# Softmax shares transposed in 32x32 blocks on VectorE and regrouped through DRAM, with query tiles of every fourth 32 tokens

## Chip, cores and metric

The kernel runs on one core of a Trainium2 chip. The metric is its device time in microseconds, as the median of repeated runs; a profiled execution of the same program supplies the trace. Five engines work side by side, each with a queue of its own that is worked off in order: PE (matmuls; its weight loads are listed apart as PEld), DVE (VectorE), ACT (ScalarE), POOL (GpSimd) and SP (SyncE, which issues nearly all DMAs).

## What is computed

One layer of a hybrid encoder, in fp32: 512 tokens with 16 meta tokens put ahead of them, width 2048. Cut to what matters:

```python
hn   = rmsnorm(h, pre_norm_g)                       # (528, 2048)
proj = einsum('bld,dc->blc', hn, w_in)              # w_in: 2048 x 6656
qa, ka, va, ga, qb, kb, vb, gb = split(proj)

# mixer A: 8 heads of 128 on 2 key/value heads, RMSNorm on q and k, axial rotary
s  = einsum('bkgqd,bksd->bkgqs', qa, ka) * scale
ya = softmax(s) @ va * silu(ga)

# mixer B: 8 heads, two softmaxes of 64 columns each, with a distance penalty
bias = -slope[h] * abs(qpos[:, None] - kpos[None, :])
a  = softmax(q1 @ k1.T * scale + bias) - lam * softmax(q2 @ k2.T * scale + bias)
yb = rmsnorm(a @ vb, subln_g) * (1 - lambda_init) * silu(gb)

y = einsum('blc,cd->bld', concatenate([ya, yb]), w_out)   # 2048 x 2048
return (h + rmsnorm(y, post_norm_g))[:, 16:, :]           # the 512 tokens
```

## The kernel before

**Numbers.** Every product of fp32 numbers is made of three products of shorter numbers: an operand x is split into `hi` (a copy with rounding on ACT, L335) and `lo` = x - hi (a subtraction on DVE, L338), and hi·hi, lo·hi and hi·lo are summed in PSUM. So one piece of work on PE is a triple of matmuls, recorded by the helper behind L61; transposes on PE are recorded by the one behind L64.

**Order.** The object `Lanes` (L42 to L103) writes PE's instructions in program order and keeps a clock of estimated microseconds. Attention is written as generators ("tasks"): each `yield` of a number asks to be continued so many estimated microseconds later, the numbers standing in the table `LAG` (L32). After each triple of the projection, `poll` lets one task that is due write its PE instructions. So PE's queue is projection work with attention's scores, transposes and products with V strewn in at chosen distances. Other engines are ordered by a scheduler, by priority; weight splits get a high one (L153 to L159). On SP the loads are kept in the order in which they are written.

**Weights.** `wload` takes a block of 128 x 1024 of w_in from DRAM into a staging buffer `st` (L149), from where ACT writes `wh` (L156) and DVE `wl` (L157). The pool has three buffers of each. In the background SP and POOL move blocks of w_out and sum them in DRAM (`ws`; `load` at L141, and accumulating DMAs that POOL issues at L785); the projection behind attention uses these sums to need fewer products. At the end `wlast` loads four blocks of w_out that are used as they are.

**Attention.** A query tile is 128 tokens in a row: `q[:, tq]`. For each head there are two halves of two tiles. Mixer B (`attention_B`, L484 to L526) and mixer A (`attention_A`, L573 to L615) do the same with one tile: scores into the PSUM tile `sc` (one buffer); DVE takes scale and distance and finds the row's extreme into `p` (L502, L601); ACT takes the exponential and the row's sum (L510, L604); DVE its reciprocal (L512, L605); POOL scales p by it (L515, L606); in B, DVE adds the second softmax with its weight (L517). The distance comes from one table `dist`, read at an offset `w0` that depends on the tile. `p` is 128 queries x 528 keys, and has six buffers; `room` holds a task back while they are taken.

**Products with V.** The product needs the shares the other way round, keys on the partitions. `p_times_v` (L437 to L479) has PE transpose each p: per half, eight transposes of 128 x 128 for the 512 tokens and two of 32 columns for the 16 meta keys, in three PSUM banks `tr`. From PSUM, ACT writes `ph` (L335) and DVE `pl` (L338), each in two pieces of 512 columns; the meta keys' shares go to `pm`, where POOL makes a copy of the hi part. Then come 13 matmuls of 256 queries: three for each of the four 128-token blocks of keys, and one for the meta keys. The two transposing banks and the products are separate steps with lags between them (`turnA/B`, `bankA/B`, `pvA/B`), and the whole task starts a lag `pA` or `pB` after the scores.

**End.** The output projection works in blocks of columns for two token tiles at a time; `third_done` closes one tile's third block, `last_block` the last one's, and `row_block` scales a block, adds the residual and stores it. `end` does this for the last two tiles, t = 0 and t = 1.

Of the kernel before, what the change touches and what calls it, by code (L numbers as in the profile page):

```python
# [31 lines left out]
LAG = dict(vals=3.5, bank=2.8, bankA=1.5, bankB=2.5, turnA=1.5, turnB=1.5, pvA=2.6, pvB=4.0, scB=3.0,  # L32
           pB=8.0, ss=6.0, qA=2.35, scA=5.4, pA=4.14, rope=10.2, head=3.85, fin=1.35, qn=1.4, norm=4.0, valsA=(10.0, 7.0),
# [73 lines left out]
def kernel(ctx: ExitStack, tc: tile.TileContext, xT, xn, xm, w_s, w_t, w_q, w_o,  # L107
# [78 lines left out]
    def xload(k):  # L186
        st = ap.tile([P, NT], F32, name="xs", tag="p", bufs=6)
# [165 lines left out]

    dist = ap.tile([P, DW], F16, name="dist", tag="dist", bufs=1)
    pad(ap, "dpad", 32)
    load(dist, dist_d[2])
# [4 lines left out]
    def queries_B(h, pss, after=nullcontext):  # L361
# [7 lines left out]
        l2 = ap.tile([P, SEQ], F32R, name="l2", tag="ql", bufs=4)  # L369
        with after():  # L370
            hi(q1[L], qf[L])
            hi(q2[U], qf[U])
            hi(q1[U], qf[L])
            hi(q2[L], qf[U])
            lo(l1[L], qf[L], q1[L])
            lo(l2[U], qf[U], q2[U])
            lo(l1[U], qf[L], q1[L])
            lo(l2[L], qf[U], q2[U])
# [36 lines left out]
    pv_last, p_live = [None], [0]  # L415
# [15 lines left out]
    def room(n):  # L431

        while p_live[0] + n > 6:
            yield 0.3
        p_live[0] += n

    def p_times_v(pts, v, done, gate_of):  # L437
# [3 lines left out]
        ph = ap.tile([P, TT, 2 * P], F32R, name="ph", tag="ph")  # L441
        pl = ap.tile([P, TT, 2 * P], F32R, name="pl", tag="pl")
        pm = ap.tile([96, 2 * P], F32R, name="pm", tag="pm")
        for b in range(2):
            if b:
                yield LAG["turn" + ab]
            tr = ptr.tile([P, 512], F32, name="tr", tag="tr")
            for i in range(2):
                c = NM + (2 * b + i) * P
                for j in range(2):  # L450
                    transpose(tr[:, (2 * i + j) * P:(2 * i + j + 1) * P],
                                        pts[j][:, c:c + P], ident)
            tv = tr.rearrange("p (c q) -> p c q", c=2)
            hi(ph[:, 2 * b:2 * b + 2, :], tv)
            lo(pl[:, 2 * b:2 * b + 2, :], tv, ph[:, 2 * b:2 * b + 2, :])
        yield LAG["bank" + ab]
        tr = ptr.tile([P, 512], F32, name="tr", tag="tr")
        for j in range(2):
            transpose(tr[:32, j * P:(j + 1) * P], pts[j][:, 0:32], ident)
        p_live[0] -= 2 * len(pts) if gate_of is None else len(pts)  # L460
        hi(pm[0:32], tr[0:32, :2 * P])
# [17 lines left out]
        done(o)  # L479

# [3 lines left out]
    def attention_B(h, qs, ks, v, v_task):  # L484
        o = ap.tile([P, SEQ], F32, name="oB", tag="f", bufs=4)
        last = None
        for half in range(2):
            pts = []
            for t in (2 * half, 2 * half + 1):
# [4 lines left out]
                yield from room(2)  # L494
# [709 lines left out]
```

## Time and profile before

| what | value |
|---|---|
| time, median of 3 runs | 916.49 us (916.39 to 916.67) |
| profiled execution: time / span | 915.9 us / 914.1 us |
| mean granted TensorE clock | 0.997 |
| DMA: bytes, mean rate | 149.86 MB, 164 GB/s |
| share of 16 DMA engines, SP's queue / POOL's queue | 43.2% / 10.8% |
| DRAM read / written | 140.55 MB / 41.94 MB |

How to read it: busy time is the sum of the instructions' durations, overlaps counted once. A matmul's duration is longer than the time by which it holds up the next one, since matmuls are pipelined; what one costs is read from the distance between starts. In a row of groups, the numbers behind the first bar are busy us and mean ns of one, and behind the second the idle time of the engine ahead of them, with what ended it. Rows of instructions have the start in us and the duration in us.

### The profile page before, as it was taken

To read this page: it belongs to the slowest core of one execution; us is meant where nothing else is said; L and a number is where in the kernel's file an instruction comes from. 1 tells how busy PE (TensorE), PEld (TensorE's weight loads), DVE (VectorE), ACT (ScalarE), POOL (GpSimd) and SP (SyncE) were. 2 spreads that over 40 slices of the span, in tenths; PEclk is the share of its full clock that TensorE was granted. 3 is DMA by queue.
4 is the path that set the end of the run, shared out by engine and by line. 5 is a ranking of instruction groups with operands and counts; after the bars stand their busy time and mean duration, and the time that the engine had idled before them with its cause. 6 is when DMAs were issued, how large, how long until landed. Compare 5 with 4: busy or idle time off the path is not lost.

```text
span 914.1 us, 14275 instructions
## 1 busy us (share of the span) xinstructions
PE 900.1 (98%) x5450; PEld 799.6 (87%) x5450; DVE 587.9 (64%) x1041; ACT 503.1 (55%) x877; POOL 121.3 (13%) x168
## 2 busy tenths in 40 slices
PE   9999999999999999999999999999999999999995
PEld 8999898998989989898998888998888888888884
DVE  6586675757557485575765374686554665876887
ACT  6565564737456384554744434565566565665552
POOL 0101111210201111011010011231111100000012
PEclk9999999999999999999999999999999999999998
DMA  9837636674848658484322332133212228979784
GB/s 338 288 125 205 166 124 174 175 187 128 236 129 206 175 159 217 117 237 124 102 73 70 104 106 79 48 104 115 82 58 93 81 81 287 304 260 323 251 250 176
DMA packets 52979, 149.86 MB, mean 164 GB/s; under 512 B 7920, under 2 KB 14960, under 8 KB 52528
## 3 DMA queue, kind: packets, MB, share of 16 engines
q1 hardware_dynamic: 48160, 132.18, 43.2%
q0 software_dynamic: 4608, 16.78, 10.8%
q8 instruction: 42, 0.69, 0.3%
q14 instruction: 25, 0.20, 0.1%
q10 hardware_dynamic: 144, 0.01, 0.0%
HBM read 140.55 MB, written 41.94 MB: 200 GB/s over the span
## 4 chain that ended last, share of the span: by engine, by line
PE 91%; DVE 5%; ACT 2%; issue 1%; DMA 1%; DVEq 0%; ACTq 0%
PE pd L61 60%; PE po L61 14%; PE sc L61 6%; PE pv L61 5%; PE tr L64 5%; DVE wl L157 1%; DVE y L1102 1%; DMA st<-in_w_o_dram 1%; PE hot L61 0%; PE ss L61 0%; DVE y L1026 0%; DVE p L601 0%; ACT wh L156 0%; DVE l L338 0%; DVE pl L338 0%
## 5 line engine op out<-in xcount | busy, mean ns | idle before, releaser
L61 PE MATMUL pd<-xh,wh 128*128 128x264 f32 (+1 forms) x992 | 333.7, 336 | 0.0
L61 PE MATMUL pd<-xl,wh 128*128 128x264 f32 (+1 forms) x992 | 323.4, 326 | 0.0
L61 PE MATMUL pd<-xh,wl 128*128 128x264 f32 (+1 forms) x992 | 323.3, 326 | 0.0
L156 ACT ACTIVATE wh<-st 128x1024 fp32r<-128x1024 f32 (+2 forms) x159 | 165.6, 1041 | 200.3 <-PE pd L61 76.4
L157 DVE TENSOR_TENSOR wl<-st,wh 128x1024 fp32r<-128x1024 f32 (+2 forms) x159 | 191.1, 1203 | 106.2 <-ACT wh L156 105.1
L61 PEld LDWEIGHTS pd<-xh,wl 128*128 128x128 f32 x992 | 186.6, 188 | 16.3 <-DVE wl L157 0.2
L61 PEld LDWEIGHTS pd<-xh,wh 128*128 128x128 f32 x992 | 187.1, 189 | 11.1 <-ACT wh L156 0.3
L61 PEld LDWEIGHTS pd<-xl,wh 128*128 128x128 f32 x992 | 187.6, 189 | 9.5
L510 ACT ACTIVATE p<-p,mx 128x528 f32<-128x528 f32 x64 | 46.9, 734 | 43.2 <-DVE mx L502 42.9
L338 DVE TENSOR_TENSOR pl<-tr,ph 128x512 fp32r<-128x512 f32 x64 | 43.3, 685 | 15.2 <-ACT ph L335 14.8
L64 PE MATMUL tr<-ident,p 128*128 128x128 f32 (+1 forms) x320 | 50.6, 272 | 1.8 <-DVE pl L338 0.7
L502 DVE CUSTOM_DVE_ANT_0 p<-sc,dist 128x528 f32<-128x528 f32 x64 | 44.9, 701 | 11.4 <-PE sc L61 11.0
L61 PE MATMUL pd<-wh,xh 128*128 128x512 f32 x128 | 51.1, 399 | 0.0
L61 PE MATMUL pd<-wl,xh 128*128 128x512 f32 x128 | 50.0, 391 | 0.0
L61 PE MATMUL pd<-wh,xl 128*128 128x512 f32 x128 | 49.9, 390 | 0.0
L335 ACT ACTIVATE ph<-tr 128x512 fp32r<-128x512 f32 x64 | 37.5, 590 | 21.3 <-PE tr L64 20.9
L64 PEld LDWEIGHTS tr<-ident,p 128*128 128x128 f32 (+1 forms) x320 | 36.9, 131 | 12.0 <-DVE pl L338 1.1
L517 DVE SCALAR_TENSOR_TENSOR p<-p,c 128x528 f32<-128x528 f32 x32 | 24.5, 766 | 31.6 <-POOL p L515 31.6
L785 POOL DMA_DIRECT2D ws<-in_w_o_dram x32 | 26.7, 834 | 123.3 <-DMA ws<-in_w_o_dram 66.1
L606 POOL TENSOR_SCALAR p<-p,smA 128x528 f32<-128x528 f32 x32 | 23.1, 721 | 137.6 <-DVE smA L605 99.3
L604 ACT ACTIVATE p<-p,mxA 128x528 f32<-128x528 f32 x32 | 23.5, 736 | 31.8 <-DVE mxA L601 31.1
L515 POOL TENSOR_SCALAR p<-p,sm 128x528 f32<-128x528 f32 x32 | 22.8, 714 | 137.1 <-DVE sm L512 126.1
(221 smaller groups left out, 1591.1 us busy)
## 6 DMA issues: line engine op xcount, KB each, us to landing
st<-in_w_t_dram SPq DMA_DIRECT2D x82, 512.0 KB, 4.3
ws<-in_w_o_dram POOLq DMA_DIRECT2D x32, 512.0 KB, 8.1
st<-ws SPq DMA_DIRECT2D x32, 512.0 KB, 4.3
st<-in_w_o_dram SPq DMA_DIRECT2D x24, 512.0 KB, 4.4
ws<-in_w_o_dram SPq DMA_DIRECT2D x16, 512.0 KB, 6.5
ws<-ws SPq DMA_DIRECT2D x16, 512.0 KB, 5.4
st<-in_w_q_dram SPq DMA_DIRECT2D x16, 512.0 KB, 3.5
xs<-in_xT_dram SPq DMA_DIRECT2D x16, 264.0 KB, 5.2
```

Of the source, the lines that this page charges most:

```text
L61: self._add(self.nc.tensor.matmul(out, lhsT, rhs, start=start, stop=stop, **kw), us)
L64: self._add(self.nc.tensor.transpose(out, in_, ident), 0.109)
L156: splits.append((nc.scalar.activation(wh[:, c], st[:, c], AF.Copy), nc.vector.tensor_tensor(out=wl[:, c], in0=st[:, c], in1=wh[:, c].bitca ...
L157: nc.vector.tensor_tensor(out=wl[:, c], in0=st[:, c], in1=wh[:, c].bitcast(F32), op=ALU.subtract)))
L335: nc.scalar.activation(dst, src, AF.Copy)
L338: nc.vector.tensor_tensor(out=dst, in0=src, in1=h.bitcast(F32), op=ALU.subtract)
L502: nc.vector.tensor_tensor_reduce(out=two(p), in0=sc[:, :, :HALF], in1=two(dist[:, w0:w0 + NT]), scale=-0.125 / slope(h), scalar=3.0e38, op ...
L510: nc.scalar.activation(p2[m], p2[m], AF.Exp, scale=-1.0, bias=mx[:, m:m + 1], accum_out=sm[:, m:m + 1])
L517: nc.vector.scalar_tensor_tensor(out=p2[0], in0=p2[1], scalar=c2, in1=p2[0], op0=ALU.mult, op1=ALU.add)
L604: nc.scalar.activation(p, p, AF.Exp, scale=-1.0, bias=mx, accum_out=sm)
L606: nc.gpsimd.tensor_scalar(out=p, in0=p, scalar1=sm, scalar2=1.0, op0=ALU.mult, op1=ALU.mult)
L785: nc.gpsimd.dma_start(out=dst, in_=src, accum_op=ALU.add)
```

## The change

**What it does.** PE no longer transposes p. As soon as a p is scaled, `turned` has DVE transpose it in square blocks of 32 x 32: one instruction for the 512 tokens' columns (L448 of the changed kernel) and one for 32 columns that hold the meta keys (L450), both into `pt`, a tile of 128 x 1088 for the two tiles of a half, with one buffer. Transposing inside blocks leaves the blocks themselves where they are, so `regroup` sends pt to DRAM (`turn`, three buffers, L455) and fetches it back in five pieces that put 32 partitions each in their place (L461 four times into `pl`, L462 into `pmf`). `p_times_v` then splits what came back from SBUF: `ph` in one piece of 1024 columns on ACT, `pl` in place on DVE.

To make the pieces long, a query tile now holds every fourth group of 32 tokens. q is written in that order (`dealt`, `by_token`), `dist` is loaded in four pieces of 32 partitions that are shifted by 96 columns each, and its offset moves by 32 per tile. The 256 queries of a product lie in four runs of 64 columns in ph and pl, and the result is put back in the order of tokens as ACT copies it out (`half_of`, `by_quad`).

The table of lags changes with it: the products with V come later behind the scores (`pA`, `pB`, `pvA`, `pvB`). p has four buffers in place of six, `room` is gone, and the buffers of `xs` at the start are taken from two tags. At the end, two blocks of w_out are loaded early (`come_early`) and split early (`split_early`); `third_done` takes both tiles, with subtractions and squares ahead of the gains; and the last row block of t = 0 is moved behind the last subtraction of t = 1.

```diff
-LAG = dict(vals=3.5, bank=2.8, bankA=1.5, bankB=2.5, turnA=1.5, turnB=1.5, pvA=2.6, pvB=4.0, scB=3.0,
-           pB=8.0, ss=6.0, qA=2.35, scA=5.4, pA=4.14, rope=10.2, ...
+LAG = dict(vals=3.5, bank=2.8, bankA=1.5, bankB=2.5, turnA=1.5, turnB=1.5, pvA=5.5, pvB=6.0, scB=3.0,
+           pB=14.0, ss=6.0, qA=2.35, scA=5.1, pA=11.5, rope=10.2, ...
...
-    load(dist, dist_d[2])
+    for i in range(4):
+        rows = slice(32 * i, 32 * i + 32)
+        load(dist[rows, 96 * i:], dist_d[2, rows, :DW - 96 * i])
+
+    def by_token(t):
+        return t.rearrange("p (i t q) -> p i t q", i=4, t=TT)
+
+    def dealt(t):
+        return t.rearrange("p (t i q) -> p i t q", i=4, t=TT)
+
+    def half_of(t, half):
+        return t.rearrange("p (i h r) -> p i h r", i=4, h=2)[:, :, half]
...
-    def room(n):
-        while p_live[0] + n > 6:
-            yield 0.3
-        p_live[0] += n
-
-    def p_times_v(pts, v, done, gate_of):
+    def turned(pt, p, j):
+        nc.vector.transpose(pt[:, :1024].rearrange("p (m c t q) -> p c m t q", m=4, c=TT, t=2)[
+            :, :, :, j], p[:, NM:].rearrange("p (c m q) -> p c m q", c=TT, m=4))
+        nc.vector.transpose(pt[:, 1024 + 32 * j:1056 + 32 * j], p[:, :32])
+
+    def regroup(pt):
+        turn = dr.tile([P, 1088], F32, name="turn", tag="turn", bufs=3)
+        nc.sync.dma_start(out=turn, in_=pt)
+        turn = turn.rearrange("(i k) r -> k i r", i=4)
+        pl = ap.tile([P, 1024], F32R, name="pl", tag="pl")
+        pm = ap.tile([32, 2 * P], F32, name="pmf", tag="pmf", bufs=1)
+        quad = pl.bitcast(F32).rearrange("p (i r) -> p i r", i=4)
+        for m in range(4):
+            nc.sync.dma_start(out=quad[32 * m:32 * m + 32], in_=turn[:, :, 256 * m:256 * m + 256])
+        nc.sync.dma_start(out=pm.rearrange("p (i r) -> p i r", i=4), in_=turn[:, :, 1024:])
+        return pl, pm
+
+    def p_times_v(regrouped, v, done, gate_of):
...
-        for b in range(2):
-            if b:
-                yield LAG["turn" + ab]
-            tr = ptr.tile([P, 512], F32, name="tr", tag="tr")
-            for i in range(2):
-                c = NM + (2 * b + i) * P
-                for j in range(2):
-                    transpose(tr[:, (2 * i + j) * P:(2 * i + j + 1) * P],
-                                        pts[j][:, c:c + P], ident)
...
-            hi(ph[:, 2 * b:2 * b + 2, :], tv)
-            lo(pl[:, 2 * b:2 * b + 2, :], tv, ph[:, 2 * b:2 * b + 2, :])
...
+        pl, pf = regrouped
+        ph = ap.tile([P, 1024], F32R, name="ph", tag="ph")
+        pm = ap.tile([96, 2 * P], F32R, name="pm", tag="pm", bufs=1)
+        pt = pl.bitcast(F32)
+        hi(ph, pt)
+        lo(pl, pt, ph)
+        hi(pm[0:32], pf)
...
+        ph, pl = [t.rearrange("p (i c r) -> p c i r", i=4, c=TT) for t in (ph, pl)]
...
-                    w0 = (TT - 1 - t) * P
+                    w0 = 3 * P - 32 * t
...
-                pts.append(p2[0])
+                turned(pt, p2[0], t % 2)
...
-        hi(qh, tr)
-        lo(ql, tr, qh)
+        hi(dealt(qh), by_token(tr))
+        lo(dealt(ql), by_token(tr), dealt(qh))
...
-    second(1, pd2, held[1][1], None)
+    def come_early(i):
+        if i < 2:
+            early[i] = yp.tile([P, 1024], F32, name="wr", tag=f"wr{i}")
+            load(early[i], block(1, 1, 1, i))
+    second(1, pd2, held[1][1], come_early)
...
+        for t in (t0, t0 + 1):
+            by_gain(t, 3)
+            part(t)
...
     def end(u, ps):
         last_block(u, ps)
+        if u:
+            row_block(0, GS[3])
         order(by_gain(u, 2))
         turned(u)
-        for g in (0, 3, 1, 2):
+        for g in GS[:4 if u else 3]:
             row_block(u, g)
```

**PE, in a head of mixer B.** The first place is in the middle of B, in the projection's work between two steps of attention; `pd` is the projection's PSUM tile, `xh` and `xl` the input's halves. Before:

```order
L61 MATMUL pd<-xh_115,wh 128x512
L61 MATMUL pd<-xl_131,wh 128x512
L61 MATMUL pd<-xh_115,wl 128x512
L64 MATMUL tr<-ident,p 128x128 [waits Activation_49]
L64 MATMUL tr<-ident,p 128x128 [waits DVE_49]
L64 MATMUL tr<-ident,p 128x128 x2
L61 MATMUL pd<-xh_116,wh 128x512
L61 MATMUL pd<-xl_132,wh 128x512
```

And in the changed kernel:

```order
L61 MATMUL pd<-xh_116,wh 128x512
L61 MATMUL pd<-xl_132,wh 128x512
L61 MATMUL pd<-xh_116,wl 128x512
L61 MATMUL pd<-xh_117,wh 128x512
L61 MATMUL pd<-xl_133,wh 128x512
L61 MATMUL pd<-xh_117,wl 128x512
```

The four transposes with their two waits are gone, and one triple follows the next.

**DVE, at the end of a head of mixer B.** The second place is DVE's queue from the second half's last reciprocal on (`sm`: the row sums; `vm`, `vl`: pieces of V; `kf`: the next head's keys; `pl` at L338: the shares' lo part of this head). Before:

```order
L512 RECIPROCAL sm<-sm 128x2
L514 TENSOR_TENSOR c_3381<-sm,nlam 128x1
L517 SCALAR_TENSOR_TENSOR p<-p,c_3381 128x528
L338 TENSOR_TENSOR vm<-tr,vm 16x128
L329 TENSOR_TENSOR kf<-pd,rB 128x264 x2
L157 TENSOR_TENSOR wl<-st,wh 128x1024
L338 TENSOR_TENSOR s_3465<-kf,s_3465 64x528
L338 TENSOR_TENSOR s_3466<-kf,s_3466 64x528
L338 TENSOR_TENSOR pl<-tr,ph 128x512 x2
```

And in the changed kernel, where `pl` at L340 is that of the same head's first half:

```order
L529 RECIPROCAL sm<-sm 128x2
L531 TENSOR_TENSOR c_3323<-sm,nlam 128x1
L534 SCALAR_TENSOR_TENSOR p<-p,c_3323 128x528
L340 TENSOR_TENSOR vl<-tr,vh 128x512
L448 STREAM_TRANSPOSE pt<-p 128x4x4x32
L450 STREAM_TRANSPOSE pt<-p 128x32
L157 TENSOR_TENSOR wl<-st,wh 128x1024
L340 TENSOR_TENSOR vm<-tr,vm 16x128
L340 TENSOR_TENSOR pl<-pl,ph 128x1024
L340 TENSOR_TENSOR pm<-pmf,pm 32x256
L331 TENSOR_TENSOR kf<-pd,rB 128x264 x2
L157 TENSOR_TENSOR wl<-st,wh 128x1024
```

The two block transposes follow the scaled p, and the first half's split, which stood ahead of this place, now stands behind them, with a weight split (L157) between.

**SP, in a head of mixer B.** The third place is SP's queue, which held only weight loads and w_out's sums. Before:

```order
L149 DMA st<-in_w_t_dram 128x1024 [waits DMAHW0_49,DVE_49]
L149 DMA st<-in_w_t_dram 128x1024 [waits DMAHW1_49,DVE_49]
L149 DMA st<-in_w_t_dram 128x1024 [waits DMAHW3_49,DVE_49]
L141 DMA ws_570<-ws_566 16x8192 [waits DMAHW2_49,DMASW6_49]
L141 DMA ws_571<-ws_567 16x8192 [waits DMASW0_49]
L149 DMA st<-in_w_t_dram 128x1024 [waits DMAHW7_49,DMAHW4_49,DVE_49]
```

And in the changed kernel:

```order
L455 DMA turn<-pt 128x1088 [waits DVE_49]
L149 DMA st<-in_w_t_dram 128x1024 [waits DMAHW2_49,DMAHW1_49,DVE_49]
L461 DMA pl<-turn 32x4x256 [waits DMAHW0_49,PE_49]
L461 DMA pl<-turn 32x4x256 [waits DMAHW3_49]
L461 DMA pl<-turn 32x4x256 [waits DMAHW4_49]
L461 DMA pl<-turn 32x4x256 [waits DMAHW5_49]
L462 DMA pmf<-turn 32x4x64 [waits DMAHW6_49]
L455 DMA turn<-pt 128x1088 [waits DMAHW7_49,DVE_49]
L141 DMA ws_584<-ws_580 16x8192 [waits DMASW0_49]
L141 DMA ws_585<-ws_581 16x8192 [waits DMAHW1_49,DMASW2_49]
L461 DMA pl<-turn 32x4x256 [waits DMAHW7_49,DMAHW2_49,PE_49]
```

Weight loads and sums now share the queue with six DMAs for each half, and stand behind the waits of these: the store of pt waits for DVE, the first fetch for the store and for PE, which must be done with pl's old content.

More of the change, by code (lines that the diff above doesn't have):

```diff
@@ L369, in queries_B @@
         l2 = ap.tile([P, SEQ], F32R, name="l2", tag="ql", bufs=4)
+        to, qf = [dealt(t) for t in (q1, l1, q2, l2)], by_token(qf)
         with after():
[L371 to L378, printed above, removed]
+            hi(to[0][L], qf[L])
+            hi(to[2][U], qf[U])
+            hi(to[0][U], qf[L])
+            hi(to[2][L], qf[U])
+            lo(to[1][L], qf[L], to[0][L])
+            lo(to[3][U], qf[U], to[2][U])
+            lo(to[1][U], qf[L], to[0][L])
+            lo(to[3][L], qf[U], to[2][U])
         return (q1, l1), (q2, l2)
@@ L456, in p_times_v @@
[L456 to L461, printed above, removed]
+        pl, pf = regrouped
[3 more added lines that the diff above has]
+        hi(ph, pt)
@@ L593, in attention_A @@
                 sm = ap.tile([P, 1], F32, name="smA", tag="sm", bufs=4)
-                yield from room(1)
                 sc = psc.tile([P, 2, 512], F32, name="sc", tag="sc")
@@ L607, in attention_A @@
                                         op0=ALU.mult, op1=ALU.mult)
-                pts.append(p)
+                turned(pt, p, t % 2)
                 if t % 2 == 0:
                     yield LAG["scA"]
-            last = spawn_pv(v_task, p_times_v(pts, v, lambda pv, half=half: nc.scalar.activation(
-                oA[h][:, half * 256:(half + 1) * 256], pv, AF.Copy), h), LAG["pA"])
+            last = spawn_pv(v_task, p_times_v(regroup(pt), v, lambda pv, half=half:
+                            nc.scalar.activation(half_of(oA[h], half), by_quad(pv), AF.Copy), h),
+                            LAG["pA"])
             if half == 0:
@@ L792, in otile @@
         return xtile(name, n, dt)[:, NM:NT]
+    early, early_ws = {}, {}
     def wlast(i):
-        st = wp.tile([P, 1024], F32, name="st", tag="st")
-        nc.sync.dma_start(out=st, in_=block(1, 1, 1, i))
+        if i in early_ws:
+            return early_ws[i]
+        if i in early:
+            st = early[i]
+        else:
+            st = wp.tile([P, 1024], F32, name="st", tag="st")
+            nc.sync.dma_start(out=st, in_=block(1, 1, 1, i))
         ws = []
@@ L801, in wlast @@
             src = st[:, j * 512:(j + 1) * 512]
-            with tc.high_priority(rank[0]):
+            with tc.high_priority(0 if i in early else rank[0]):
                 hi(wh, src)
@@ L1113, in turned, with third_done, split_early @@
         order(nc.vector.reciprocal(out=ry[t], in_=ry[t]))
-    def third_done(t, ps):
-        TTv(out=y[t][3], in0=ps, in1=y[t][3], op=SUB)
-        square(t, 3, y[t][3])
-        by_gain(t, 3)
-        part(t)
-    ry = {}
-    third = [product(of_t(t3), banks(pd), beside=lambda i: residual())]
-    for u, ps in enumerate(third[0]):
-        third_done(2 + u, ps)
-    third.append(product(of_t(t3), banks(pd2), beside=lambda i: residual()))
+    def third_done(t0, pss):
+        for u, ps in enumerate(pss):
+            v = y[t0 + u][3]
+            TTv(out=v, in0=ps, in1=v, op=SUB)
+            square(t0 + u, 3, v)
+        for t in (t0, t0 + 1):
+            by_gain(t, 3)
+            part(t)
+    def split_early(i):
+        with tc.issue_after(splits[-3][0].ins), tc.issue_after(splits[-3][1].ins):
+            early_ws[i] = wlast(i)
+    ry, GS = {}, (0, 3, 1, 2)
+    third = [product(of_t(t3), banks(pd), beside=lambda i: (residual(), i == 3 and split_early(0)))]
+    third_done(2, third[0])
+    third.append(product(of_t(t3), banks(pd2),
+                         beside=lambda i: (residual(), i == 1 and split_early(1))))
     for u, ps in enumerate(third[1]):
```

45 lines of the change are left out of this document (22 added, 23 removed).

## The prediction

> **What bounds the kernel now.** I read the page from the top: busy times, then the chain that ended last, then the list of PE's own waits, because a busy PE is not yet a PE without gaps.
>
> ```profile
> span 914.1 us, 14275 instructions
> PE 900.1 (98%) x5450; PEld 799.6 (87%) x5450; DVE 587.9 (64%) x1041; ACT 503.1 (55%) x877; POOL 121.3 (13%) x168
> ...
> PE 91%; DVE 5%; ACT 2%; issue 1%; DMA 1%; DVEq 0%; ACTq 0%
> PE pd L61 60%; PE po L61 14%; PE sc L61 6%; PE pv L61 5%; PE tr L64 5%; DVE wl L157 1%; DVE y L1102 1%; DMA st<-in_w_o_dram 1%; PE hot L61 0%; PE ss L61 0%; DVE y L1026 0%; DVE p L601 0%; ACT wh L156 0%; DVE l L338 0%; DVE pl L338 0%
> ```
>
> 91% of the chain is PE, and 5% of it are transposes. These are the three waits of PE in the view of waits that stand before a transpose of p; the other rows of that view add up to 1.7 us more, 1.2 of it at the start:
>
> ```profile
> PE tr L64 <- DVE pl L338: 0.7, 1, 0.7
> PE tr L64 <- DVE qlA L338: 0.7, 1, 0.7
> PE tr L64 <- ACT oA L611: 0.3, 1, 0.3
> ```
>
> So PE is issued back to back from its first matmul to its last, and every PE slot that is taken out shortens the kernel by that slot, as long as PE's inputs keep up. The windows show the room on the others (columns: PE, PEld, DVE, ACT, POOL busy, granted clock, DMA share, GB/s), in the middle of mixer B and of mixer A:
>
> ```profile
> 205.00:260.00 55.00, 55.00 (x372) 50.67 (x371) 35.16 (x64) 30.77 (x49) 8.24 (x11) 1.00 0.65 177
> 650.00:700.00 50.00, 50.00 (x292) 43.04 (x291) 26.60 (x53) 30.33 (x50) 8.64 (x13) 1.00 0.24 80
> ```
>
> **Removed from PE.** All transposes of p are gone; those of q, k and v stay.
>
> ```profile
> L64 PE MATMUL tr<-ident,p x320: 270/272/329, 78.1 to 751.5; 128*128 128x128 f32 x128, 128*32 128x128 f32 x32
> ...
> 289.33 0.29 PE L61 MATMUL pd<-xh,wl 128*128 128x264 f32 x1
> 289.46 0.60 PE L64 MATMUL tr<-ident,p 128*128 128x128 f32 x4
> 289.81 0.37 PE L61 MATMUL pd<-xh,wh 128*128 128x264 f32 x1
> 290.02 0.29 PE L61 MATMUL pd<-xl,wh 128*128 128x264 f32 x1
> ```
>
> A duration of 272 ns is not what one costs, since matmuls overlap; the starts tell. From 289.46 to 290.02 are 0.56 us with four transposes and one matmul of 264 columns, whose slot is 0.12 (0.13 from 289.33 to 289.46). That leaves 0.44, or 0.11 each. 320 x 0.11 = **35.2 us** off PE, plus the **1.7 us** of waits above, which have no instruction left to stand before.
>
> **Added on VectorE.** 64 times a transpose of 512 columns in 32 x 32 blocks and one of 32 columns. No row shows that operation. The nearest, by columns and type, are these (the first row, a split on ACT, is used further down):
>
> ```profile
> L338 DVE TENSOR_TENSOR pl<-tr,ph 128x512 fp32r<-128x512 f32 x64 | 43.3, 685 | 15.2 <-ACT ph L335 14.8
> L156 ACT ACTIVATE wh<-st 128x1024 fp32r<-128x1024 f32 (+2 forms) x159 | 165.6, 1041 | 200.3 <-PE pd L61 76.4
> L157 DVE TENSOR_TENSOR wl<-st,wh 128x1024 fp32r<-128x1024 f32 (+2 forms) x159 | 191.1, 1203 | 106.2 <-ACT wh L156 105.1
> L649 DVE TENSOR_TENSOR qn<-qn,cosT 128x256 f32<-128x256 f32 x16 | 6.1, 417 | 0.0
> L544 DVE RECIPROCAL sq<-sq 128x128 f32<-128x128 f32 x32 | 27.1, 910 | 1.7 <-ACT sq L541 1.5
> ```
>
> I take 0.69 us for 512 columns and 0.1 for 32, 0.8 a pair. The ends are 0.42 (L649, half the columns) and 3.6 (four times L544, the slowest row per column). 64 x 0.8 = 51 us on DVE; the split of pl in one piece of 1024 gives back 2 x 685 - 1203 = 0.17 us 32 times, 5 us. DVE goes to about 634 of 880 us, 72%: it is not the bound. L649 works in runs of 32 columns and pays nothing for them against the others, so the new layouts of q, ph and pt cost nothing on DVE.
>
> [...]
>
> **Added in DRAM.** Each of 32 halves writes 557 KB and reads it back in five pieces: 35.7 MB in all. In B that is 2.2 MB per 53 us, 42 GB/s on 177, so the DMA share goes from 0.65 to about 0.80. The landing times of like transfers:
>
> ```profile
> oscr<-oA SPq DMA_DIRECT2D x8, 256.0 KB, 2.6
> ob<-oscr SPq DMA_DIRECT2D x8, 256.0 KB, 3.6
> st<-in_w_t_dram SPq DMA_DIRECT2D x82, 512.0 KB, 4.3
> ws<-in_w_o_dram POOLq DMA_DIRECT2D x32, 512.0 KB, 8.1
> ...
> 274.36 0.33 SPq L149 DMA_DIRECT2D st<-in_w_t_dram  x1
> ...
> SPq L149 <- DVE wl L157: 532.3, 123, 10.6
> ```
>
> I take 3.6 us for each leg (ob is read in the same 1 KB runs) and 5 issues of 0.33: a round trip of 8.9 us; ends 2 x 2.6 + 1.7 = 6.9 and 2 x 8.1 + 1.7 = 17.9. On SP's queue the weight loads now stand behind these issues, and behind the wait for the first leg. They have the room: the last row says that SP sits 532 us waiting for a staging buffer to come free, so its loads are early by several chunks. If a load did come late, it would show as wh waiting for st.
>
> **What of it lies on the path.** In steady B the place that is nearest to PE is the first half of each head. Its pl is subtracted on DVE behind the last transposes of the second half, as the DVE rows above show. From the trace, the end of such a head:
>
> ```profile
> 298.78 0.28 PE L61 MATMUL sc<-s,l 128*128 128x264 f32 x1
> 299.10 0.71 DVE L502 CUSTOM_DVE_ANT_0 p<-sc,dist 128x528 f32<-128x528 f32 x1 [0.56 <-PE sc L61]
> 301.63 0.16 DVE L512 RECIPROCAL sm<-sm 128x2 f32<-128x2 f32 x1
> 302.55 0.83 POOL L785 DMA_DIRECT2D ws<-in_w_o_dram  x1 [6.79 <-DMA ws<-ws]
> 304.65 0.70 POOL L515 TENSOR_SCALAR p<-p,sm 128x528 f32<-128x528 f32 x1
> 305.38 0.77 DVE L517 SCALAR_TENSOR_TENSOR p<-p,c 128x528 f32<-128x528 f32 x1 [3.41 <-POOL p L515]
> 306.18 0.28 DVE L338 TENSOR_TENSOR vm<-tr,vm 16x128 fp32r<-16x128 f32 x1
> ```
>
> In the changed order POOL scales this p before its two DMA issues, so the scaling can start at about 301.9 and not 304.65. Then POOL 0.7, L517 0.8 (to 303.5), transposes 0.8, the split wl 1.2, vm 0.3, pl 1.2: pl is there at about 307.0. PE has 69 instructions between this score and the first product with V, 8.3 us at 0.12, and asks for pl two slots later: 298.9 + 8.3 + 0.2 = 307.4. That is level; I charge 0.4 us for each of 8 heads, **+3 us**. In A the split of a half also stands behind the next half's transposes; counted in the order's rows, PE gives the first four halves some 19 us after their last scores and the later ones about 25, so I charge the first four 0.5 each, **+2 us**. Ends: 0, and 1 us more for 12 places with each us that the chain is longer.
>
> Nothing is charged for the split of q by 32-token pieces, dist in four loads, the smaller pools of p, pm and xs, and the two blocks of w_o that come early: PE waits for none of these today, and DVE and ACT have 28% and more idle there. Without that cover a late split would cost PE its own length, 1.2 us.
>
> **The end.** PE's last matmul starts at 903.26 and ends at 903.65.
>
> ```profile
> 903.26 0.39 PE L61 MATMUL po<-wl,t4h 128*128 128x512 f32 x1
> ...
> 903.38 2.74 DVE L1102 SCALAR_TENSOR_TENSOR y<-y,ssy,xr 128x512 f32<-128x512 f32 x4
> 906.03 0.68 DVE L1108 TENSOR_TENSOR y<-po,y 128x512 f32<-128x512 f32 x1
> 907.51 0.69 DVE L1026 TENSOR_TENSOR y<-y,gpB 128x512 f32<-128x512 f32 x1 [0.79 <-ACT jko L1023]
> 908.31 2.74 DVE L1102 SCALAR_TENSOR_TENSOR y<-y,ssy,xr 128x512 f32<-128x512 f32 x4
> ```
>
> L1108 of the last rows waits for four row blocks of the rows before. One of the four moves behind it, into the 0.79 us in which DVE waits for ACT: 2.74 / 4 = **0.7 us** off. The rest of the 10.45 us tail stays.
>
> **Sum.** The profiled execution took 915.9 us with a span of 914.1: 915.9 - 35.2 - 1.7 - 0.7 + 3 + 2 = 883.3. The median of the runs shown, 916.49, is 0.6 above that execution, so **883.9 us**.
>
> **Rivals.**
> 1. The shares come later than I charge: the block transposes lie some way up between 0.8 and their upper end, or DVE's in-order queue holds them. Each us costs 12; a chain that is 0.5 to 1.5 us longer gives 883.9 + 6 to 18 = 890 to 902. For: the margin in B is level. Against: DVE has 28% idle. [...]
> 2. Slower than before: the way through DRAM. The last p of a first half in B is done at 291.85:
>
> ```profile
> 291.08 0.77 DVE L517 SCALAR_TENSOR_TENSOR p<-p,c 128x528 f32<-128x528 f32 x1 [1.51 <-POOL p L515]
> ```
>
> With 0.8 us of transposes it can leave at 292.7, and the splits (hi 1.0, lo 1.2) need it 2.3 us before 307.4, so a round trip of up to 12.4 us is free; beyond that each us costs 8, one per head. The gain of 32.6 is used up at 12.4 + 4.1 = 16.5 us. With both legs at the slowest row, 17.9, it is 883.9 + 8 x 5.5 = 928. For: a DMA share of 0.80 in B, and the 8.1 us of POOL's transfers. Against: like transfers on SP's queue take 2.6 to 4.3.
> 3. PE reads ph and pl in runs of 64 columns instead of 256 in a row. Today a product with V takes a slot of 0.12:
>
> ```profile
> 299.26 0.28 PE L61 MATMUL pv<-ph,vh 128*128 128x256 f32 x1
> 299.38 0.28 PE L61 MATMUL pv<-ph,vl 128*128 128x256 f32 x1
> ```
>
> No row shows a moving operand in runs on PE. At half rate 384 matmuls would cost 0.12 more each: 883.9 + 46 = 930; it eats the gain from 71% of that price on. [...]
> 4. It does not do what it says: another engine takes over and the time stays at 916.5. Against: PE's list of waits is nearly empty.
>
> **How the numbers follow.** Forecast, 879 to 890 (no new waits; waits of 11): 0.60. Rival 1: 0.20. Rival 2: 0.06. Rival 3: 0.05. Rival 4: 0.03. Below 879, or some other small loss above 902: 0.06. The range takes the first two: 878 to 902. A change of 0.2%, 1.8 us, is about what a measurement of this kernel can tell. Faster by more: 0.87; within: 0.03; slower: 0.10.
>
> **What would show it.** Right: no transposes of p on PE, the block transposes near 0.69 and 0.1 us, DVE near 634 us, PE's waits with pv behind pl of a few us in all, the tail from PE's last matmul at 9.8. Wrong: pv matmuls 0.24 apart (rival 3), pl waiting long for turn (rival 2), block transposes above 1.2 us or p on DVE late so that sc waits (rival 1).

## The result, and the profile after

The changed kernel is slower: 952.88 us as the median of 4 runs (949.57 to 957.57) against 916.58 for the kernel before (916.39 to 916.83), a ratio of 1.0404 with a 95% interval of 1.0376 to 1.0432. The forecast was 883.9 us with a range up to 902. The profiled execution took 949.57 us.

The page of the changed kernel, in the same rows as before, with the group of the new operation and two rows of the DMA issues (number, KB each, median us to landing):

```profile
span 947.8 us, 14079 instructions
PE 888.2 (94%) x5130; PEld 782.6 (83%) x5130; DVE 631.9 (67%) x1137; ACT 497.1 (52%) x845; POOL 130.2 (14%) x168
...
PE 60%; DMA 14%; DVE 12%; ACT 6%; issue 4%; POOL 2%; SPq 2%; DVEq 0%; ACTq 0%; POOLq 0%
...
L448 DVE STREAM_TRANSPOSE pt<-p 128x512 f32<-128x512 f32 x64 | 45.3, 707 | 30.3 <-DMA turn<-pt 18.9
...
turn<-pt SPq DMA_DIRECT2D x32, 544.0 KB, 3.1
...
pl<-turn SPq DMA_DIRECT2D x128, 128.0 KB, 4.0
```

PE has 320 matmuls less, as the change says, but is busy only 11.9 us less (888.2 against 900.1), not the 35.2 of the transposes; most of that difference is the clock, as shown below. And it now stands idle for 947.8 - 888.2 = 59.6 us, where it was 14.0. These two make up the whole 33.7 us of span: 45.6 - 11.9. The chain that ended last, 91% PE before, now has 14% DMA. The median landing times are as good as forecast (3.1 and 4.0 us), so it is not the usual transfer that costs.

PE's own list of waits (us in total, times, longest):

```profile
PE pv L61 <- ACT ph L337: 13.3, 6, 3.5
PE pv L61 <- DVE pl L340: 10.6, 12, 2.5
PE sc L61 <- DVE mx L519: 8.6, 11, 3.1
PE pd L61 <- ACT wh L156: 6.4, 1, 6.4
```

The products with V wait for the shares, the scores for DVE, and one chunk of the projection for its weights. Where these stand shows in the chain, here followed back through one head of mixer B (start, us, what):

```profile
247.95 0.84 POOL ws L803
...
252.23 9.29 DMA turn<-pt
...
261.59 0.33 SPq L461
...
262.90 2.77 DMA pl<-turn
...
265.77 1.07 ACT ph L337
...
266.86 1.24 DVE pl L340
...
268.14 1.11 PE pv L61 x4
```

Read from above: POOL issues a sum of w_out at 247.95 (and, as its other rows show, a second one at 249.21). At 252.23 the first half's pt is sent to DRAM and takes 9.29 us to land instead of 3.1. Only then can SP issue the fetch, ACT and DVE split, and PE multiply. From 213 to 270 us, about a head, the DMA share is 0.71, but in the first 6 us of that store it is 1.00 (the number before the last; the last is GB/s):

```profile
252.20:255.20 3.00, 3.00 (x27) 3.00 (x27) 2.74 (x8) 1.78 (x3) 0.70 (x1) 1.00 1.00 147
255.20:258.20 3.00, 3.00 (x28) 3.00 (x27) 1.42 (x3) 1.43 (x3) 0.00 (x0) 1.00 1.00 289
```

Three engines stand still behind it:

```profile
261.62 0.71 DVE L448 STREAM_TRANSPOSE pt<-p 128x512 f32<-128x512 f32 x1 [5.00 <-DMA turn<-pt]
...
265.77 1.06 ACT L337 ACTIVATE ph<-pl 128x1024 fp32r<-128x1024 f32 x1 [4.69 <-DMA pl<-turn]
...
266.88 0.39 PE L61 MATMUL pv<-ph,vh 128*128 128x256 f32 x1 [3.46 <-ACT ph L337]
```

And there is a second bill. The windows of the stretch before the wait's end, of the one behind it and of the next (columns as in the prediction; the number behind the last bracket is the granted clock):

```profile
263.40:266.80 3.40, 0.03 (x1) 0.00 (x0) 3.37 (x6) 1.03 (x2) 0.00 (x0) 1.00 0.56 180
268.20:271.50 3.30, 3.30 (x16) 3.30 (x17) 0.42 (x1) 0.00 (x0) 0.31 (x2) 0.51 0.96 309
271.70:275.00 3.30, 3.30 (x22) 3.02 (x22) 1.29 (x3) 1.97 (x3) 1.29 (x2) 1.00 1.00 233
```

PE idles for 3.4 us. From 268.2, 1.3 us after it resumes, it gets half its clock for some 3.3 us, and only then the full one: 16 matmuls instead of 22. Over the run the mean granted clock fell from 0.997 to 0.978, which is 0.019 x 947.8 = 18 us. The same trace has half clock behind a shorter wait too, one of 2.10 us: the 3.4 us that begin 0.85 us after that wait's end have a clock of 0.50:

```profile
206.05 0.39 PE L61 MATMUL pv<-ph,vh 128*128 128x256 f32 x1 [2.10 <-ACT ph L337]
...
206.90:210.30 3.40, 2.99 (x14) 2.99 (x15) 0.86 (x2) 0.00 (x0) 1.03 (x2) 0.50 0.71 225
```

By stage, DVE's last minimum over a score of mixer B starts at 499.0 us, before it was 465.7 (forecast: some 15 us earlier). So mixer B alone lost 33 us. In mixer A the last one starts at 766.9 instead of 728.6: another 5 us lost, where 16 were to be won.

### The profile page after: what moved, and what is told of

It is laid out like the page before. It is cut to its first block, busy times and chain, and to the rows that moved or that the text cites. A ratio compares the mean times of both kernels' runs of the same rounds, so it can differ in the third digit from the quotient of the medians.

```text
span 947.8 us, 14079 instructions
## 1 busy us (share of the span) xinstructions
PE 888.2 (94%) x5130; PEld 782.6 (83%) x5130; DVE 631.9 (67%) x1137; ACT 497.1 (52%) x845; POOL 130.2 (14%) x168
## 4 chain that ended last, share of the span: by engine, by line
PE 60%; DMA 14%; DVE 12%; ACT 6%; issue 4%; POOL 2%; SPq 2%; DVEq 0%; ACTq 0%; POOLq 0%
PE pd L61 36%; PE po L61 15%; DMA turn<-pt 7%; PE pv L61 4%; DMA pl<-turn 4%; PE sc L61 4%; DVE sq L562 2%; DVE wl L157 2%; ACT ph L337 1%; DMA st<-in_w_t_dram 1%; DVE pt L448 1%; SPq L461 1%; DVE pl L340 1%; DMA ws<-in_w_o_dram 1%; DMA ws<-ws 1%
## 5 line engine op out<-in xcount | busy, mean ns | idle before, releaser
L61 PE MATMUL pd<-xl,wh 128*128 128x264 f32 (+1 forms) x992 | 327.4, 330 | 0.4 <-DVE xl L192 0.4
L157 DVE TENSOR_TENSOR wl<-st,wh 128x1024 fp32r<-128x1024 f32 (+2 forms) x159 | 191.4, 1205 | 101.4 <-ACT wh L156 100.4
L61 PEld LDWEIGHTS pd<-xh,wh 128*128 128x128 f32 x992 | 190.4, 192 | 19.7 <-ACT wh L156 6.8
L448 DVE STREAM_TRANSPOSE pt<-p 128x512 f32<-128x512 f32 x64 | 45.3, 707 | 30.3 <-DMA turn<-pt 18.9
L61 PE MATMUL pv<-ph,vh 128*128 128x256 f32 x128 | 38.5, 301 | 16.0 <-ACT ph L337 13.3
L519 DVE CUSTOM_DVE_ANT_0 p<-sc,dist 128x528 f32<-128x528 f32 x64 | 44.7, 698 | 11.7 <-PE sc L61 11.6
L340 DVE TENSOR_TENSOR pl<-pl,ph 128x1024 fp32r<-128x1024 f32 x32 | 39.5, 1233 | 17.4 <-ACT ph L337 17.2
L337 ACT ACTIVATE ph<-pl 128x1024 fp32r<-128x1024 f32 x32 | 33.6, 1049 | 32.0 <-DMA pl<-turn 32.0
L61 PE MATMUL pv<-pl,vh 128*128 128x256 f32 x128 | 39.3, 307 | 10.6 <-DVE pl L340 10.6
L476 POOL TENSOR_SCALAR pm<-pm 32x256 fp32r<-32x256 f32 x32 | 29.0, 906 | 134.9 <-ACT pm L337 98.7
L61 PE MATMUL sc<-s,q 128*128 128x264 f32 x128 | 35.7, 299 | 11.4 <-DVE mx L519 8.6
```

Of the source, the lines that this page charges most:

```text
L61: self._add(self.nc.tensor.matmul(out, lhsT, rhs, start=start, stop=stop, **kw), us)
L157: nc.vector.tensor_tensor(out=wl[:, c], in0=st[:, c], in1=wh[:, c].bitcast(F32), op=ALU.subtract)))
L337: nc.scalar.activation(dst, src, AF.Copy)
L340: nc.vector.tensor_tensor(out=dst, in0=src, in1=h.bitcast(F32), op=ALU.subtract)
L448: nc.vector.transpose(pt[:, :1024].rearrange("p (m c t q) -> p c m t q", m=4, c=TT, t=2)[:, :, :, j], p[:, NM:].rearrange("p (c m q) -> p ...
L519: nc.vector.tensor_tensor_reduce(out=two(p), in0=sc[:, :, :HALF], in1=two(dist[:, w0:w0 + NT]), scale=-0.125 / slope(h), scalar=3.0e38, op ...
```

## The experiments

Where no interval is given, a number is one run, beside one of the kernel before on the same chip (915.9 to 917.1). The four runs of the changed kernel lie 8 us apart, so a few us between two single runs say little, and the waits in the traces say more.

**1. Without the sums, with more lag, with two buffers, without DRAM.** The theory at this point: the sums of w_out, which POOL issues as accumulating DMAs, hold the DMA engines; a store of pt that meets them is late. Its rival: the single buffer of pt, or SP's order, stalls DVE by itself.

no_sums:

```diff
-                nc.gpsimd.dma_start(out=dst, in_=src, accum_op=ALU.add)
+                pass
```

> Leaves out the 32 accumulating DMAs that POOL issues (L803), so the summed blocks of w_out hold only their first term; all else as in the changed kernel. Theory 1 (these sums hold the 16 DMA engines, the store of pt that is issued among them lands after 9 us instead of 3, and the wait goes on to DVE, ACT and PE): the store lands in about 3 us in every half, PE's waits in mixer B go from some 45 us to under 10, the granted clock goes back above 0.99, and the time falls from 953 to 890 - 905. Theory 2 (the single buffer of pt, or the order on SP's queue, stalls DVE and PE by itself): waits and time stay near the changed kernel's, above 935.

Measured: 916.86 us. In the views of the tile pt, of the changed kernel and of this one, the longest landing of the store falls, the median stays:

```profile
DMA to landing us min/median/max: 2.7/3.1/9.4
```

```profile
DMA to landing us min/median/max: 2.7/3.1/5.2
```

PE's waits for ph are gone altogether, 36 us of the loss with them:

```profile
PE sc L61 <- DVE mx L519: 8.9, 12, 3.1
PE pv L61 <- DVE pl L340: 6.5, 8, 2.5
PE pd L61 <- ACT wh L156: 6.4, 1, 6.4
```

So the sums are what delays the store. But the run also frees POOL, which in the changed kernel waits 117.6 us (60.2 + 57.4) ahead of its sums, so the 36 us need not be the store's delay alone. The time is not the 890 to 905 expected, and the clock (0.985) is not above 0.99: these three waits stay, and they are not the sums' transfers. Of the 69 us between the forecast and the changed kernel the sums are about half.

lagB:

```diff
-           pB=14.0, ...
+           pB=20.0, ...
```

> Only the lag pB, from the scores of a half of mixer B to its split and product, goes from 14 to 20 estimated us. Theory 1: the 13.5 us round trip is then covered, ACT and PE wait less for the fetch (ph and pl together 24 us before, now under 8); DVE's wait for the store stays: 915 to 935. Theory 2 (single buffer): DVE's wait and so the rest stay: above 940.

Measured: 918.86 us, inside the range expected. ph is waited for no more, pl in 3 places for 2.0 us; the scores' waits are 10.9 us (8.6 in the changed kernel). Two things have changed for ph. PE comes to the products later: 18.4 us behind the store's issue (254.93 against 236.56), where it asked after 11.2. And the store is fast again, though all the sums run: the stores at 236.6 and 244.4 us stand between sums that are issued at 222.0 and 252.6. In the view of pt from 170 to 445 us, of the changed kernel and of this one:

```profile
DMA to landing us min/median/max: 3.0/5.3/9.4
```

```profile
DMA to landing us min/median/max: 3.1/3.2/4.9
```

The run does not tell what each of the two is worth.

pt2:

```diff
-            pt = ap.tile([P, 1088], F32, name="pt", tag="pt", bufs=1)
+            pt = ap.tile([P, 1088], F32, name="pt", tag="pt", bufs=2)
...
-        ph = ap.tile([P, 1024], F32R, name="ph", tag="ph")
+        ph = ap.tile([P, 1024], F32R, name="ph", tag="ph", bufs=1)
```

> Gives pt two buffers; to make room ph has one instead of two, and two of the tiles that the input is squared in at the start take pt's buffers. Theory 1 (the sums delay the store): DVE no longer waits 18.9 us for the store, so the scores' waits (sc for mx, 8.6 us) shrink, but the products with V still wait for the round trip: 938 to 950. Theory 2 (the single buffer is the cause): PE's waits in mixer B are gone, 885 to 905.

Measured: 958.69 us, outside what both theories had. This speaks against the rival: with two buffers of pt (and one of ph, which can cost too) DVE waits for pt no more, but the store still takes up to 9.9 us, and PE's waits for ph rise to 19.8 us. DVE's wait of 5 us for the store is a consequence, not the cause.

direct16:

```diff
-        turn = dr.tile([P, 1088], F32, name="turn", tag="turn", bufs=3)
-        nc.sync.dma_start(out=turn, in_=pt)
...
+        for i in range(4):
+            for m in range(4):
+                nc.sync.dma_start(out=quad[32 * m:32 * m + 32, 256 * i:256 * i + 256],
+                                  in_=pt[32 * i:32 * i + 32, 256 * m:256 * m + 256])
+            nc.sync.dma_start(out=pm[:, 64 * i:64 * i + 64], in_=pt[32 * i:32 * i + 32, 1024:])
```

> No way through DRAM: 20 DMAs per half from pt straight to pl and pmf in SBUF, 16 of 32 x 256 and 4 of 32 x 64 numbers. One leg and 17.8 MB of traffic less, 15 issues more per half on SP (about 6 us). Theory 1: the one leg is still delayed by the sums where it meets them, but the chain is shorter by the fetch (about 4 us): products with V wait under 10 us in all, 900 to 930. Theory 2 (single buffer): pt is held as long as before or longer, 940 and above.

Measured: 1038.16 us, a clear miss, in the range that the rival had (940 and above). pt is held longer too: DVE waits 60.4 us for it, where it was 18.9. The run is therefore not evidence against the rival. What holds pt here is the number of issues; their row (ns of one, min/median/max):

```profile
L459 SPq DMA_DIRECT2D pl<-pt x512: 507/589/2022, 75.1 to 875.3; - x171
```

The 16 issues into pl take 0.59 us each at the median, not the 0.33 to 0.43 of the larger ones. With the 4 into pmf at the same price (an estimate from this row) that is 12 us of SP's queue per half, and 23% of the chain is SP.

**2. POOL's queue, SP's queue, the end.** adds2 issues each sum one step later behind the copy that it adds to:

```diff
-            if adds:
+            if len(adds) > 1 or adds and not steps:
```

> The changed kernel, with each accumulating DMA of POOL issued one step later behind the copy it adds to (two copies ahead instead of one), so that POOL's queue does not stand waiting for the copy with a scaling of p behind it; lags as in the change (pB 14). Theory 1 in its first form (the sums' transfers on the DMA engines delay the store): the sums still run, a little later; time 935 to 955. Theory 3 (POOL's own waits, by which p is scaled late and sums and store are issued at the same moment, are the main part): below 920.

Measured: 953.95 us. This does not test POOL's own waits, since the edit leaves them as they were: POOL stands 117.0 us (61.0 + 56.0) ahead of its sums, and 117.6 in the changed kernel. What these waits are worth by themselves stays open.

adds2_lagB is both edits.

> Both: pB 20 and the sums one step later. If the scores' waits that remain with pB 20 (10.9 us in 8 places and three stretches at half clock) come from POOL's sum that waits for its copy ahead of the scaling of p, they fall below 4 us and the time goes from 918.9 to 902 - 909. If they come from the store or the fetch, 915 to 920.

Measured: 914.65 us, with 11.1 us of scores' waits left. The expectation of under 4 us failed, and here too POOL's waits are as in lagB (95.7 us against 95.8). What makes the scores' waits shows in lagB, in rows of POOL, DVE and PE of one head:

```profile
394.83 0.81 POOL L803 DMA_DIRECT2D ws<-in_w_o_dram  x1 [11.01 <-DMA ws<-in_w_o_dram]
395.72 0.70 POOL L532 TENSOR_SCALAR p<-p,sm 128x528 f32<-128x528 f32 x1
```

```profile
396.46 0.77 DVE L534 SCALAR_TENSOR_TENSOR p<-p,c 128x528 f32<-128x528 f32 x1 [5.41 <-POOL p L532]
397.14 0.70 DVE L519 CUSTOM_DVE_ANT_0 p<-sc,dist 128x528 f32<-128x528 f32 x1
```

```profile
397.91 0.59 PE L61 MATMUL sc<-s,q 128*128 128x264 f32 x1 [3.34 <-DVE mx L519]
```

POOL waits 11 us before it can issue the third sum in a row, for the copy that SP issued at 383.12 and that takes 11.2 us to land. The scaling of p stands behind that issue, DVE's L534 behind the scaling, the next minimum behind L534, and PE's next score behind that minimum, since sc has one buffer. Each in-order queue holds the next one.

both adds a later issue of the fetch of pmf:

```diff
+        pf = ap.tile([32, 2 * P], F32, name="pmf", tag="pmf", bufs=1)
+        nc.sync.dma_start(out=pf.rearrange("p (i r) -> p i r", i=4), in_=turn[:, :, 1024:])
+        yield 4.0
```

> As adds2_lagB, and the fetch of the meta keys' shares (pmf, one buffer) is issued 4 estimated us ahead of its split instead of right behind the fetch of pl, so that SP's queue does not stand waiting for DVE's last use of pmf with weight loads behind it. If that wait is what makes wh late at the end of mixer A (6.4 us, and then 10 us at half clock), the gain over adds2_lagB is 8 to 12 us: 892 to 900. If ACT's wait for the fetch of pl is the cause, no change against adds2_lagB (within 3 us).

Measured: 926.00 us, outside both expectations. The wait of 6.4 us for wh in mixer A is gone (2.9 us come later, in the output projection), but the fetch now comes too late: PE waits 8.6 us for pm, 7.2 of it in one place. A trade, not a gain.

end_only:

> The kernel before with the end part of the change alone: two blocks of w_out loaded and split early, third_done over two tiles, the row block of t = 0 behind the last subtraction. The prediction had 0.7 us off; the changed kernel's tail behind PE's last matmul is 1.8 us shorter than before's. Expected: 914.5 to 916.1.

Measured: 913.70 us, 3.05 below its neighbour, a little more than expected, but one pair of runs. From the end of PE's last matmul to the end of the span are 8.4 us instead of 10.45, so the end part is good by itself.

**3. Fewer sums at a time, two buffers of pmf.** spread has three steps of the sums per head instead of five:

```diff
         if h > 0:
-            weigh(2)
+            weigh()
...
+    weigh(2)
     kA = keys_A(pss)
+    weigh(2)
...
         for k0 in range(0, KT, 2):
+            weigh()
             wh, wl = fetch()
```

> The changed kernel with its own lags; the same 32 sums, but three steps per head of mixer B instead of five, the rest in the stretch of projection work behind mixer B (about 500 to 590 us), in which no shares go through DRAM. Theory 1 (sums that run while pt is stored): if a single sum at the moment of the store is enough to delay it, little changes (940 to 955); if it is the row of two or three sums in a row, the store of a first half lands in under 6 us and the time falls to 920 - 935.

Measured: 927.95 us, 25 us of the loss gone with the lags of the change, in the range of the theory of sums in a row. From 170 to 445 us the store takes at most 7.5 us instead of 9.4, the median is 3.7 instead of 5.3; under 6 was expected. The last head of mixer B, where two pairs remain, waits 7.5 us for ph.

> As spread, with pB 20. With pB 20 the scores' waits (10.9 us and three stretches at half clock) came where POOL scales p behind the last of three sums. With one sum at a time POOL is free sooner: these waits fall under 5 us, 903 to 911. If they have another cause, 915 to 920.

Measured: 907.88 us. The scores' waits are 6.0 us, of which 4.9 stand at that same last head.

pmf2:

```diff
-        pm = ap.tile([32, 2 * P], F32, name="pmf", tag="pmf", bufs=1)
+        pm = ap.tile([32, 2 * P], F32, name="pmf", tag="pmf", bufs=2)
```

> The changed kernel with pB 20 and two buffers of pmf instead of one (room from the unused first 288 columns of dist and from small tiles), so that SP's fetch of pmf no longer waits for DVE's use of the one before it with weight loads behind it. If this wait makes wh late at the end of mixer A (6.4 us, then some 10 us at half clock), 918.9 becomes 905 to 912 and that wait is gone; if not, 916 to 920 with the wait still there.

Measured: 907.37 us, and the wait for wh of 6.4 us is still there. So the gain of 11.5 us against lagB comes from other places (the scores' waits are 3.1 instead of 10.9 us), and the theory on SP's wait for pmf fell. SP's rows ahead of that wait show what else stands in the way of the weight loads:

```profile
686.65 0.34 SPq L454 DMA_DIRECT2D turn<-pt  x1
...
690.03 1.75 SPq L460 DMA_DIRECT2D pl<-turn  x4
...
692.29 0.43 SPq L149 DMA_DIRECT2D st<-in_w_t_dram  x1
697.91 0.34 SPq L454 DMA_DIRECT2D turn<-pt  x1
698.29 1.61 SPq L149 DMA_DIRECT2D st<-in_w_t_dram  x1
```

The weight load of 698.29 stands behind a store whose pt is ready only at 697.9: SP waits 5 us for it. No weight load goes out between 678 and 692. But this is not what PE waits for. The loads of 692.29 and 698.29 land 4.5 and 5.8 us after their issue, the later one at 704.1. ACT splits them at 708.63, at least 4.5 us later, since other work (a table load, a gate's function, ph, p) stands ahead in its own order:

```profile
703.41 1.28 ACT L579 ACT_TABLE_LOAD   x1 [1.78 <-DVE gt L578]
...
705.24 1.04 ACT L336 ACTIVATE ph<-pl 128x1024 fp32r<-128x1024 f32 x1
...
708.63 1.99 ACT L156 ACTIVATE wh<-st 128x1024 fp32r<-128x1024 f32 x2
```

So ACT's order makes the 6.4 us here. Whether the scheduler chose this order because of SP's late loads, no run shows.

combo is spread and pmf2 together.

> All three: pB 20, sums spread, pmf in two buffers. If each removes its own wait, the gains add up: 890 to 902, below both kernels.

Measured: 914.51 us, a miss. At the last head of mixer B, where the two pairs of sums are, a score waits 4.3 us, and the mean granted clock is 0.985, where pmf2 has 0.993.

**4. Single sums, and weight loads out of the stores' way.** prio is pmf2 with high priority for the weight loads in SP's order:

```diff
-            dma(out=st[:, c], in_=src if parts == 1 else src[:, c])
+            with tc.high_priority(rank[0]):
+                dma(out=st[:, c], in_=src if parts == 1 else src[:, c])
```

> As pmf2 (pB 20, pmf in two buffers), and the weight loads get the same high priority as their splits in the order of SP's queue. pmf2 kept the 6.4 us wait for wh at the end of mixer A, and its trace has no weight load on SP between 679 and 692 us while loads of ob, stores of pt and their waits stand there. If weight loads that stand behind waiting stores are the cause, that wait goes, with the half clock behind it: 896 to 902 against 907.4. If the cause is ACT's own order, within 2 us of 907.4.

Measured: 912.69 us. The wait left its place and came back in two others:

```profile
PE pd L61 <- ACT wh L157: 7.7, 2, 4.5
```

combo2 is combo without the pairs:

```diff
-    weigh(2)
     kA = keys_A(pss)
-    weigh(2)
```

> As pmf2, with three steps of the sums per head of mixer B and the rest one at a time in the two stretches of query projections of mixer A (no pairs, so none in a row while mixer B's last head still runs, which cost 4.4 us in combo). If single sums leave the store and the scaling of p alone: 899 to 904. If sums in the query projections meet mixer A's first heads: 907 to 912.

Measured: 903.04 us, inside the first range; six later runs of it (below) have a median of 907.52, at the edge of the second, so the two expectations are not told apart. And combo3, with the priority of prio:

> combo2 and prio together: 890 to 897 if both hold, and then no wait of PE over 1.5 us is left outside the start.

Measured: 906.80 us, a miss: the waits for wh are the 7.7 us of prio. Against combo2 this one run tells no difference, since it lies inside that kernel's six.

actq takes the weight loads of mixer A's last stretch off SP's queue:

```diff
+    wq[0] = nc.scalar.dma_start
     for h in range(NH):
         if h == 5:
...
+    wq[0] = nc.sync.dma_start
     gate_7 = silu_A(gates[NH - 1])
```

> The kernel of combo2 once more, timed in rounds against the kernel before: 902 to 907, a ratio of 0.984 to 0.990. If half-clock stretches fall differently from run to run, its times spread more than those of the kernel before (which spread by 0.5 us).

> combo2, with the weight loads of the last stretch of mixer A issued on ACT's queue instead of SP's, so that none stands behind a store or fetch of the shares that waits. With high priority on SP the wait for wh only moved (7.7 us in two places instead of 6.4 in one). If SP's queue and its waits are the cause, the waits of PE for wh in mixer A go altogether (under 1.5 us) and the time is 6 to 10 us below combo2: 893 to 898. If ACT's own order is the cause, they stay: 902 to 907.

Measured: combo2 907.52 us (6 runs, 905.93 to 911.41), ratio 0.9907, interval 0.9886 to 0.9927, so somewhat less gain than expected. actq 895.85 us (5 runs, 894.85 to 898.43), ratio 0.9785, interval 0.9768 to 0.9803, both against 916.06 (11 runs). PE's waits in actq:

```profile
PE sc L61 <- DVE qlA L342: 3.0, 1, 3.0
PE pv L61 <- DVE pl L342: 1.5, 3, 0.7
PE sc L61 <- DVE l L342: 1.4, 6, 0.2
PE sc L61 <- DVE mx L521: 1.4, 6, 0.2
```

The wait for wh is gone, and 11.7 us against combo2 with it. This fits the theory of SP's queue but does not show it, since the edit changes two things: a load that ACT issues also takes a place in ACT's order, and ACT now splits one block at a time (at 693.13 and at 701.79) instead of two in a row behind other work. The rows of pmf2 speak for the order. **actq is faster than both kernels**: 20 us below the one before, and 57 below the change as it was made.

## Why the prediction was wrong, step by step

- **PE is the bound, and every slot taken out shortens the kernel as long as its inputs keep up.** Right in itself; its condition failed. No transposes of p are left.
- **The block transposes.** Right: 0.707 us for 512 columns (0.69 taken) and, in rows of the trace such as the one at 262.25, 0.17 for 32 (0.1 taken). DVE is busy 631.9 us (634 forecast).
- **Rival 3, PE reading in runs of 64 columns.** Void. Products with V that wait for nothing, in the changed kernel, start 0.12 us apart as before:

```profile
731.15 0.28 PE L61 MATMUL pv<-pl,vh 128*128 128x256 f32 x1
731.26 0.28 PE L61 MATMUL pv<-ph,vh 128*128 128x256 f32 x1
```

- **"I take 3.6 us for each leg ... a round trip of 8.9 us."** This is the step that failed. It is right for the median leg (3.1 and 4.0 us) and wrong for the halves that matter: the first halves of mixer B meet POOL's sums. There the store alone takes 9.29 us, and from the store's issue at 252.23 to the split's start at 265.77 are 13.5 us. The upper end of 17.9 was taken from POOL's transfers as if they were only slow themselves; that a transfer on SP's queue lands late among them (9.29 us) was not asked. The forecast looked at a mean DMA share (0.80 in B); it came out lower (0.71 over this head), and still the engines were full (a share of 1.00) in the first 6 us of the store. no_sums shows that the sums delay the store, and spread and lagB from the other sides.
- **"A round trip of up to 12.4 us is free."** Too much. PE asks at about 263.4, 11.2 us behind the store's issue; with 2.3 us for the splits 8.9 are free. Of the 3.5 us that are missing, 1.1 lie between p and the store: p is done at 250.35 and the store goes at 252.23, 1.9 us later and not 0.8, because a weight split (L157, 1.22 us) stands between. The other 2.4 are about what POOL was late with p, 2.3 us (the next point but one).
- **"Beyond that each us costs 8."** Too little. The wait of PE of 3.46 us is followed by 3.3 us at a clock of 0.51, and DVE and ACT stand still behind the same store and its fetch (5.00 and 4.69 us in the rows above). The scores wait 8.6 us for DVE besides; with 8.9 us in no_sums, the late store is not shown to be their cause. Rival 2, to which the forecast gave a chance of 0.06, was thus the right mechanism, priced at 928 for a trip of 17.9 us; it came with a trip of 13.5 and cost more.
- **"In the changed order POOL scales this p before its two DMA issues."** Right for that p, a second half's last (its scaling at 262.56 follows its row sum at once). But the first half's last p, on which the store hangs, has its row sum at 246.25 and is scaled only at 248.56, behind the issue of a sum at 247.95 for which POOL waited 8.58 us. With pB 20 a sum that waits does stand ahead of a scaling, and that is what the remaining waits of the scores were (lagB, and spread_lagB without it).
- **"They have the room" (weight loads on SP).** Not so in mixer A: the loads lose their lead behind stores and fetches that wait (5 us ahead of the load of 698.29 in pmf2). But the sign that the forecast named, wh waiting for st, is not what costs there: in pmf2 the blocks had landed at least 4.5 us before ACT came to them. The 6.4 us of PE and the half clock behind them come from ACT's order, which the forecast did not ask about; with actq they are gone.
- **The end.** Right in kind, too small: between the end of PE's last matmul (938.72 + 0.39) and the end of the span are 8.7 us, 1.75 less than before, against 0.7 forecast. DVE's last subtraction now starts 0.3 us behind PE, where it was 2.4 (906.03 - 903.65):

```profile
938.72 0.39 PE L61 MATMUL po<-wl,t4h 128*128 128x512 f32 x1
...
939.40 0.69 DVE L1139 TENSOR_TENSOR y<-po,y 128x512 f32<-128x512 f32 x1
```

Open is the rest. actq's profiled execution took 894.85 us. By the forecast's own terms, 915.9 - 35.2 for the transposes and - 1.75 for the end give 879.0. PE's waits by the list add up to 10.2 us instead of 3.4, and the clock of 0.993 costs 3.6: 889.4. Some 5 us are not found in the lists. Most of them show when PE's matmuls are read from start to start. The list counts a wait from the end of the matmul before, 0.28 us behind its start, while the next could have started after 0.12. By the starts, the 20 listed waits of actq behind the first 10 us cost 12.4 us and not 9.1 (in the kernel before 5 waits, 3.2 and not 2.3), and 8 shorter ones that the list leaves out cost 1.8. These are 4.2 of the 5 us.

## What to carry to other kernels

A transfer's price is that of the moment (here 9.3 us for a store that took 3.1 at the median): before a transfer is put on a path that something waits for, look at what else the DMA engines and the issuing queue do in that stretch, not at the median landing time. Work moved off the bottleneck engine onto a longer way needs its slack in the schedule in the same edit; here one lag from 14 to 20 was worth 34 us, and it moved the stores away from the sums as well. And where a wait lands on an in-order queue (a sum that waits ahead of a scaling, softmax steps ahead of a weight split), everything behind it pays, up to the engine that one wanted to free: in lagB a wait of 11.0 us on POOL became one of 3.34 us on PE.

## What was not expected of the hardware

- Behind two accumulating DMAs of POOL's queue, issued at 247.95 and 249.21, the store of 252.23 (557 KB, SP's queue) took 9.3 us instead of 3.1 at the median; without the sums the longest was 5.2 (no_sums). SP issued weight loads at 251.51 and 256.02 too, and no run here shows what they add.
- A wait of PE of 3.4 us cost nearly half as much again, through 3.3 us at a granted clock of 0.51. One of 2.1 us was followed by 3.4 us at 0.50 as well.
- DMA issues of 32 x 256 numbers between parts of SBUF took 0.59 us of SP each at the median, more than those of 512 KB, which took 0.33 to 0.43.
